# One core, a hybrid encoder layer: the order of long products, the buffers and the queues of its first stage

## The chip, the core and the metric

The kernel runs on one NeuronCore of a Trainium2 chip. The core's engines are TensorE (PE in the profile; PEld is its weight load), VectorE (DVE), ScalarE (ACT), GpSimd (POOL) and SyncE (SP). Each works through its own instructions in a fixed order and waits on semaphores for the others. SP does nothing but issue DMA copies here; POOL issues some, too, and computes beside them. The metric is the device time of one execution in microseconds, and the text compares medians of several executions.

## What is computed

One layer over a sequence of 2048 frames of width 1024. One input projection feeds two heads, their outputs are normalised and projected together, and a SwiGLU feed-forward part follows:

```python
h = rmsnorm(x, norm_mix_g[l])
proj = h @ w_in[l]
u_ssm = proj[..., :D_SSM]
q = proj[..., D_SSM:D_SSM + D_ATT]
...
y_ssm = s5_mixer(u_ssm, ...)
y_att = chunked_attention(q, k, v, attn_rel_bias[l])
mixed = jnp.concatenate([rmsnorm(y_ssm, ...), rmsnorm(y_att, ...)], axis=-1)
x = x + mixed @ w_out[l]
h2 = rmsnorm(x, norm_ffn_g[l])
x = x + (jax.nn.silu(h2 @ w_gate[l]) * (h2 @ w_up[l])) @ w_down[l]
return rmsnorm(x, norm_final_g)
```

The state-space head discretises a diagonal complex system first: `lam_bar = exp(lam * dt)`, with `b_bar`, powers of `lam_bar` and products of those powers with the matrices B and C. These tables depend on parameters alone. The attention head adds a learned bias that is clipped by distance; it reads it from a table of shape 8 x 128 x 640.

## The kernel before

All arithmetic is float32; each large product is made of three products of a high and a low part (`mm3`, line 144). Instructions are written with a tile framework: a builder orders them by priority (program order, moved by `high_priority`) and by its own estimate of when their inputs are there, allots buffers and sets the waits. A pool with `bufs=n` for a name gives n buffers in turn; the next user of one waits until all readers of the last are done. `keep_in_program_order` pins an instruction behind the one that was written just before it on its engine. All products of PE in this part are pinned, so PE's order is that of the program. The order on DVE, ACT, POOL and SP is fixed when the kernel is built, but by the builder's estimate.

The first stage, `u_phase` (line 395), projects x onto the 512 channels of the state-space head, in four blocks b of 512 columns. `prep` (line 410) loads the eight row tiles of a block (`xt`, from `in_xp`) on SP, splits each into a high part (ACT, line 424) and a low part (DVE, line 425), and loads the rows of x once more (`xn`) for the sums of squares. For block 0 it loads the weights as well. A block's four groups of 24 products on PE follow (`group`); between its first and its second group, `finish` (line 461) closes the block before: `spread_` turns the reciprocal norms into a row on PE and ACT (`pp`, `pb`), and four `evac` (line 450) multiply it in on DVE, into the buffers `us`, and store them to DRAM (`u`) on POOL's queue. The last block is closed after its fourth group.

The tables are made beside it, by the generator `ssm_prologue` (line 156), which `u_phase` and later the attention advance with `next(pro)`. Its first step issues nine loads on POOL's queue, its second computes the small tables on DVE (`exp_`, `poly`, sine and cosine, 128 x 16 elements each). Then come eight long products (`cmul`, line 267): four of 128 x 576 (`v`, stored to `vs` on POOL's queue) and four of 128 x 512 (`wt0`, `wt1`; called `wt` in the profile, as the copies below are). Each consists of six DVE operations of which two are pinned. LONG says how many of these steps follow the evacuation of blocks 0, 1 and 2: one, two and two; the other three follow the evacuation of block 3. After them POOL raises the table `a8` to powers, SP loads `bb` (`bbg`) and `v` back (`vg`, two of them in buffers called `bst`), and PE makes the kernels `kt` from them (`pp<-vg,bbg`), in program order among the first products of the attention.

The bias table (`nbms`, lines 484 to 488) is a copy from DRAM to DRAM of 8 x 128 rows of 2560 B, out of `nbs`, and two small copies that write 1e30 into corners; SP issues them in block 2. Attention reads it as `nb`.

The attention (`att_phase`, line 623) follows. Its pool `aw` lies where the first stage's pools lay. It loads and splits weights (`load_w`: `raw`, `w`) and x (`hT_unit`, lines 655 to 668), and its first q/k unit is the first work of PE after the first stage (`pf`). The feed-forward part begins at about 1000 us. Among its steps `weight_steps` (line 1166) prepares w_down; it first copies four of its blocks from DRAM to DRAM, 512 KB each (`wt`, line 1201), which the last part reads at about 2250 us. Nothing holds these four copies back, and the builder puts them early on SP's queue.

Of the kernel before, what the change touches and what calls it, by code (L numbers as in the profile page):

```python
# [61 lines left out]
DG = 3  # L62
DGROUPS = (3, 3, 3, 2), (3, 3, 3)
LATER = 230
LONG = 1, 2, 2
TAILF = 9, 10, 20, 21


# [87 lines left out]
def ssm_prologue(k, ident, S):  # L156
# [3 lines left out]
    with tc.tile_pool(name="pro", bufs=1) as p:  # L160
# [20 lines left out]
        def ts(in0, s1, s2=None, op0=ALU.mult, op1=ALU.add):  # L181
            o = sm()
            if s2 is None:
                V.tensor_scalar(o[:], in0[:], s1, None, op0=op0)
            else:
                V.tensor_scalar(o[:], in0[:], s1, s2, op0=op0, op1=op1)
            return o

        def tt(a, b, op):
            o = sm()  # L190
            V.tensor_tensor(o[:], a[:], b[:], op=op)
            return o
# [8 lines left out]
            return ts(m, MAGIC, None, ALU.subtract)  # L201

        def poly(r, cs):
            o = ts(r, cs[0], cs[1])
            for c in cs[2:]:
                o = tt(o, r, ALU.mult)
                o = ts(o, c, None, ALU.add)
            return o

        def pow2(kk):  # L210
# [5 lines left out]
        def exp_(x):  # L216
            x = ts(x, -104.0, 89.0, ALU.max, ALU.min)
            kk = rnd(x, 1.4426950408889634)
            r = stt(kk, -0.693359375, x, ALU.mult, ALU.add)
            r = stt(kk, 2.12194440e-4, r, ALU.mult, ALU.add)  # L220
            e = poly(r, [1 / 5040, 1 / 720, 1 / 120, 1 / 24, 1 / 6, 0.5, 1.0, 1.0])
            k1 = ts(kk, -100.0, 100.0, ALU.max, ALU.min)
            k2 = tt(kk, k1, ALU.subtract)
            a, b = pow2(k1), pow2(k2)
            o = sm()
            V.tensor_tensor(o[:], e[:], f32(a[:]), op=ALU.mult)
            o2 = sm()
            V.tensor_tensor(o2[:], o[:], f32(b[:]), op=ALU.mult)
            return o2
# [7 lines left out]
        r = stt(kk, -7.54978995489188216e-8, r, ALU.mult, ALU.add)  # L237
        r2 = tt(r, r, ALU.mult)
        sp = poly(r2, [2.7557319e-6, -1.9841270e-4, 8.3333333e-3, -1.6666667e-1])
        sp = tt(sp, r2, ALU.mult)  # L240
        sn = stt(sp, 1.0, r, ALU.mult, ALU.mult)
        sn = tt(sn, r, ALU.add)
        cp = poly(r2, [-2.7557319e-7, 2.4801587e-5, -1.3888889e-3, 4.1666667e-2])
        cp = tt(cp, r2, ALU.mult)
        cp = tt(cp, r2, ALU.mult)
        cs = stt(r2, -0.5, cp, ALU.mult, ALU.add)
        cs = ts(cs, 1.0, None, ALU.add)
# [118 lines left out]
        for b_ in range(4):  # L366
            nc.gpsimd.dma_start(S["kt"][:, 8 * b_ : 8 * b_ + 8, 0], kt[:])
        bb = k.t(p, "bbg", [P, NG, CH])
        nc.sync.dma_start(bb[:], S["bb"].rearrange("q g c n m -> (c n) (q g) m"))
        dm = k.t(p, "dm", [CH, NG, CH])  # L370
        V.tensor_tensor(dm[:], ident[:CH, :CH].unsqueeze(1).to_broadcast([CH, NG, CH]),
                        ddt[:].unsqueeze(2).to_broadcast([CH, NG, CH]), op=ALU.mult)
        vgs = []
        for b_ in range(4):
            vgs.append(k.t(p, "vg" if b_ < 2 else "bst", [P, 8, P], bufs=2))
            nc.sync.dma_start(vgs[b_][:], S["v"].rearrange("q g c n m -> (c n) (q g) m")[:, 8 * b_ : 8 * b_ + 8, :P])
        for b_ in range(4):
            gs = slice(8 * b_, 8 * b_ + 8)
            vg = vgs[b_]
# [15 lines left out]
def u_phase(k, ident, S):  # L395

    tc, nc, io = k.tc, k.nc, k.io
    with ExitStack() as cx:
        p2 = cx.enter_context(tc.tile_pool(name="u2", side="right", bufs=2))
        p1 = cx.enter_context(tc.tile_pool(name="u1", side="right", bufs=1))  # L400
        p3 = cx.enter_context(tc.tile_pool(name="u3", side="right", bufs=4))
        psum = cx.enter_context(tc.tile_pool(name="ups", bufs=6, space=bass.MemoryType.PSUM, reuse_waits="tile"))
        psum2 = cx.enter_context(tc.tile_pool(name="ups2", bufs=2, space=bass.MemoryType.PSUM, reuse_waits="tile"))
        k.pro_psum = psum2
        wh, wl = k.t(p1, "wuh", [P, KT, DS], F32R), k.t(p1, "wul", [P, KT, DS], F32R)
        rsn = S["rsn"][:].rearrange("p (c j) -> p j c", j=L)
        te = k.te
        X, ST, pbs = {}, {}, {}

        def prep(b, each=None):  # L410
            X[b] = []
            for q in range(KT):
                if b == 0:
                    if q % 2 == 0:
                        xn = k.t(p2, "xn", [P, D], bufs=3)
                    raw = xn[:, q % 2 * DS : q % 2 * DS + DS]
                    nc.sync.dma_start(raw, io["w_u"][q * P : (q + 1) * P, :])
                    nc.scalar.activation(wh[:, q, :], raw, AF.Copy, scale=k.gm[:, q : q + 1])
                    nc.vector.scalar_tensor_tensor(wl[:, q, :], raw, k.gm[:, q : q + 1], f32(wh[:, q, :]),
                                                   op0=ALU.mult, op1=ALU.subtract)  # L420
                xt = k.t(p3, "xt", [P, 512])
                nc.sync.dma_start(xt[:], io["xp"][q * P : (q + 1) * P, 2 * b : 2 * b + 2, :].rearrange("p j c -> p (j c)"))
                hi, lo = k.t(p2, f"hi{q}", [P, 512], F32R), k.t(p2, f"lo{q}", [P, 512], F32R)
                nc.scalar.copy(hi[:], xt[:])
                nc.vector.tensor_tensor(lo[:], xt[:], f32(hi[:]), op=ALU.subtract)
                X[b].append((hi, lo))
                if each:
                    each(q)
            ST[b] = ss = k.t(p2, "ss", [P, 4])
            for i in range(4):  # L430
                xn = k.t(p2, "xn", [P, D], bufs=3)
                nc.sync.dma_start(xn[:], io["x"].rearrange("(h p j) d -> j h p d", p=P, j=L)[2 * b + i // 2, i % 2])
                nc.scalar.activation(xn[:], xn[:], AF.Square, accum_out=ss[:, i : i + 1])

        def mm(b, f, ps, q):
            fs = slice(f * P, (f + 1) * P)
            mm3(te, ps[:], wh[:, q, fs], wl[:, q, fs], X[b][q][0][:], X[b][q][1][:], q == 0, q == KT - 1)

        def sums(b):
            with tc.high_priority():  # L440
                ST[b] = newton(k, p2, ST[b][:], D, 4)

        def spread_(b):
            ps = k.t(psum2, "pp", [P, 512])
            spread(k, te, ps, ST[b], 0)
            pbs[b] = pb = k.t(p1, "pb", [P, 512])
            nc.scalar.copy(pb[:], ps[:])
            nc.scalar.copy(rsn[:, 2 * b : 2 * b + 2, :], pb[:].rearrange("p (j c) -> p j c", j=2))

        def evac(b, f, ps):  # L450
            us = k.t(p3, "us", [P, 2, NC], bufs=2)
            nc.vector.tensor_tensor(us[:], ps[:].rearrange("p (j c) -> p j c", j=2), pbs[b][:].rearrange("p (j c) -> p j c", j=2), op=ALU.mult)
            nc.gpsimd.dma_start(S["u"][f * P : (f + 1) * P, 2 * b : 2 * b + 2, :], us[:])

        def group(b, f):
            ps = k.t(psum, "ps", [P, 512])
            for q in range(KT):
                mm(b, f, ps, q)
            return ps

        def finish(b, pss):
            with tc.high_priority():
                spread_(b)
                for f in range(4):
                    evac(b, f, pss[f])

        pss = [k.t(psum, "ps", [P, 512]) for _ in range(4)]

        def first(q):
            for f in range(4):  # L470
                mm(0, f, pss[f], q)

        pro = ssm_prologue(k, ident, S)

        next(pro)
        prep(0, first)
        with tc.high_priority(offset=-LATER):
            next(pro)
        sums(0)
        held = pss  # L480
        for b in range(1, 4):
            prep(b)
            if b == 2:
                corner = k.t(p1, "corner", [64, 64])
                nc.gpsimd.memset(corner[:], 1e30)
                nc.sync.dma_start(S["nbm"][:], bass.AP(S["nb"].tensor, S["nb"].offset + 1, [[768, H], [1, P], [1, 640]]))
                for m in range(2):
                    nc.sync.dma_start(S["nbm"][:, m * 64 : m * 64 + 64, m * 576 : m * 576 + 64].rearrange("h p c -> p h c"), corner[:].unsqueeze(1).to_broadcast([64, H, 64]))
            now = [group(b, 0)]
            finish(b - 1, held)  # L490
            for _ in range(LONG[b - 1]):
                next(pro)
            now += [group(b, 1), group(b, 2)]
            sums(b)
            held = now + [group(b, 3)]
        finish(3, held)
        for _ in range(8 - sum(LONG)):
            next(pro)
    return pro
# [666 lines left out]
def weight_steps(k, S, tile, tile1):  # L1166
# [31 lines left out]
        put(f, B22, a12)  # L1198

    for m, f in enumerate(TAILF):  # L1200
        nc.sync.dma_start(S["wt"][m], k.io["w_down"][f * P : (f + 1) * P, :])
    yield from in_turn(F2, load, first, second)


# [426 lines left out]
```

## Time and profile before

| | us |
|---|---|
| median of 3 runs | 2361.1 (2358.94 to 2367.68) |
| the profiled execution | 2359.18 |
| its span | 2357.4 |
| PE busy | 2209.4 (94%) |
| DVE busy | 1470.2 (62%) |
| POOL busy | 1140.1 (48%) |
| ACT busy | 1004.9 (43%) |
| mean clock granted to PE | 0.969 |

Times in the rows are from the start of the span. A timeline row has the start, the length, the engine, the line, the operation, output and inputs, shapes and a count; in brackets stands the idle time before it and what ended it. SPq is SP's queue: a row there is the time to issue a copy, not that of the copy. In a listing by groups stand the count, the busy time and the mean of one in nanoseconds, then the idle time before its instructions. In a list of copies stand the count, the size of one and the median from issue to landing.

### The profile page before, as it was taken

What the parts mean: (1) busy time and instruction counts of PE and PEld (TensorE: products, weight loads), DVE (VectorE), ACT (ScalarE), POOL (GpSimd) and SP (SyncE); (2) the same over time, 40 slices, a digit from 0 to 9 for tenths busy, and PEclk for the clock granted to TensorE, in tenths of its full rate; (3) what the DMA queues carried; (4) which work ended last, traced back from release to release, by engine and by line L of the source; (5) the groups of instructions that cost most, each with busy time, mean ns of one, the idle gap of its engine ahead of it and who ended that gap; (6) DMA issues with size and microseconds to landing.
All of it is one profiled execution on the core that took longest, in us unless ns stands there. A gap on an engine that the chain in (4) does not pass through costs nothing.

```text
span 2357.4 us, 30770 instructions
## 1 busy us (share of the span) xinstructions
PE 2209.4 (94%) x10712; PEld 1859.0 (79%) x10712; DVE 1470.2 (62%) x2247; ACT 1004.9 (43%) x1675; POOL 1140.1 (48%) x1284
## 2 busy tenths in 40 slices
PE   8958889999997899989999999999999989999996
PEld 6737788898986788768888887788888878888886
DVE  7554555756555845855775658766645375578676
ACT  5235545555556642333333334433333343345332
POOL 2245544556542423475555557655555464345442
PEclk9978999999998999999999999999999999999998
DMA  8876776765654434742544546654523187565541
GB/s 282 271 262 216 235 210 186 219 214 176 189 155 144 144 116 140 275 152 95 201 160 156 206 156 238 214 192 157 182 87 119 60 323 261 175 206 188 204 179 72
DMA packets 214195, 437.02 MB, mean 185 GB/s; under 512 B 27224, under 2 KB 57992, under 8 KB 206936
## 3 DMA queue, kind: packets, MB, share of 16 engines
q1 hardware_dynamic: 209176, 420.89, 53.8%
q0 software_dynamic: 4864, 14.17, 2.0%
q8 instruction: 84, 1.38, 0.2%
q14 instruction: 71, 0.58, 0.1%
HBM read 294.98 MB, written 132.15 MB: 181 GB/s over the span
## 4 chain that ended last, share of the span: by engine, by line
PE 75%; DVE 7%; DMA 7%; POOL 4%; issue 4%; ACT 2%; SPq 1%; DVEq 0%; POOLq 0%; ACTq 0%
PE X L76 19%; PE ps L76 19%; PE Y L76 9%; PE pf L76 8%; PE big L76 7%; PE W L76 5%; PE pj L76 4%; PE sc L76 2%; PE pt L79 2%; DMA xt<-in_xt 1%; DMA u<-us 1%; DMA lo<-hc 1%; DVE lo L153 1%; SPq L509 1%; DVE lo L668 1%
## 5 line engine op out<-in xcount | busy, mean ns | idle before, releaser
L76 PE MATMUL X<-hi,c 128*128 128x512 f32 x1408 | 450.6, 391 | 6.9 <-POOL c L153 3.5
L76 PE MATMUL ps<-hd,hd 128*128 128x512 f32 (+1 forms) x1968 | 433.8, 383 | 6.6 <-DVE hd L153 3.7
L76 PEld LDWEIGHTS ps<-hd,hd 128*128 128x128 f32 x1968 | 360.9, 191 | 78.2 <-DVE hd L153 4.1
L153 POOL TENSOR_TENSOR c<-S,c 128x512 fp32r<-128x512 f32 x176 | 253.1, 1439 | 240.9 <-ACT c L152 239.9
L76 PEld LDWEIGHTS X<-hi,c 128*128 128x128 f32 x1408 | 265.2, 188 | 64.2 <-POOL c L153 3.9
L153 POOL TENSOR_TENSOR hd<-hd 128x1536 fp32r<-128x1536 f32 (+1 forms) x53 | 188.7, 3568 | 208.1 <-ACT hd L152 194.3
L76 PE MATMUL X<-lo,c 128*128 128x512 f32 x704 | 274.4, 390 | 0.0
L153 POOL TENSOR_TENSOR c<-raw,c 128x512 fp32r<-128x512 f32 x132 | 190.4, 1443 | 132.7 <-ACT c L152 94.6
L152 ACT CAST hd<-hd 128x1536 fp32r<-128x1536 f32 (+1 forms) x106 | 147.4, 1393 | 225.1 <-DMA hd<-hq 154.3
L76 PE MATMUL Y<-hi,c 128*128 128x512 f32 x704 | 228.4, 395 | 13.6 <-DVE u L1320 13.6
L1444 DVE TENSOR_TENSOR acc<-acc,ps 128x512 f32<-128x512 f32 x196 | 129.1, 681 | 85.2 <-PE ps L76 85.0
L76 PEld LDWEIGHTS Y<-hi,c 128*128 128x128 f32 x704 | 134.4, 191 | 43.3 <-DVE u L1320 15.3
L76 PE MATMUL pf<-hi,w 128*128 128x512 f32 x416 | 154.3, 421 | 14.0 <-ACT hi L667 10.2
L76 PE MATMUL big<-m,woh 128*128 128x512 f32 x512 | 163.9, 402 | 0.2 <-DVE yr L986 0.2
L152 ACT CAST c<-S 128x512 fp32r<-128x512 f32 x176 | 109.4, 622 | 115.3 <-PE Y L76 59.6
L547 POOL TENSOR_TENSOR st<-X,a 128x128 f32<-128x128 f32 (+2 forms) x136 | 46.6, 343 | 229.8 <-ACT X L533 219.8
L781 DVE CUSTOM_DVE_ANT_0 s<-sc,nb 128x640 f32<-128x640 f32 (+4 forms) x128 | 94.5, 738 | 100.4 <-PE sc L76 96.3
L1316 ACT COPY u<-X 128x512 f32<-128x512 f32 x132 | 77.2, 586 | 183.7 <-PE X L76 183.7
L76 PEld LDWEIGHTS X<-lo,c 128*128 128x128 f32 x704 | 132.7, 188 | 27.6
L152 ACT CAST c<-raw 128x512 fp32r<-128x512 f32 x132 | 82.1, 622 | 152.7 <-PE Y L76 81.7
L76 PE MATMUL Y<-lo,c 128*128 128x512 f32 x352 | 138.8, 394 | 0.0
L153 DVE TENSOR_TENSOR hd<-hd 128x1536 fp32r<-128x1536 f32 (+1 forms) x53 | 114.7, 2166 | 34.0 <-ACT hd L152 33.2
(377 smaller groups left out, 4722.4 us busy)
## 6 DMA issues: line engine op xcount, KB each, us to landing
w<-wss SPq DMA_DIRECT2D x36, 1024.0 KB, 6.5
hq<-g SPq DMA_DIRECT2D x140, 256.0 KB, 2.0
hd<-hq SPq DMA_DIRECT2D x42, 768.0 KB, 4.5
hd<-wc SPq DMA_DIRECT2D x42, 768.0 KB, 6.1
raw<-in_w_gate SPq DMA_DIRECT2D x44, 512.0 KB, 3.7
raw<-in_w_up SPq DMA_DIRECT2D x44, 512.0 KB, 4.1
wc<-px SPq DMA_DIRECT2D x66, 256.0 KB, 2.7
wss<-w SPq DMA_DIRECT2D x12, 1024.0 KB, 5.3
```

The costliest lines, as they stand in the source:

```text
L76: return self.tc.keep_in_program_order(self.tc.nc.tensor.matmul(*a, **b))
L79: return self.tc.keep_in_program_order(self.tc.nc.tensor.transpose(*a, **b))
L152: nc.scalar.copy(hi, raw)
L153: (lo_eng or nc.gpsimd).tensor_tensor(lo, raw, f32(hi), op=ALU.subtract)
L509: ins = nc.sync.dma_start(out, in_)
L547: eng.tensor_tensor(t[:, :, :, :n], src, ar, op=ALU.mult)
L668: (nc.vector if sb or q % 2 == 0 else nc.gpsimd).tensor_tensor(lo[q][:], xt[:], f32(hi[q][:]), op=ALU.subtract)
L781: nc.vector.tensor_tensor_reduce(s[:, :nk].rearrange("p (a b) -> p a b", a=nch), ps[:, :nch, :half], hd.nb[:, nk - 1 :: -1].rearrange("p ( ...
L1316: nc.scalar.copy(u[:], ps[:])
L1444: V.tensor_tensor(a, a, ps[:], op=ALU.add)
```

## The change

Six edits, all but the last in the first stage:

- LONG becomes 1, 3, 4: three long products follow the evacuation of block 1, four that of block 2, none that of block 3.
- `us` has four buffers. For their room, `dm` moves into the buffer `cm1` of the long products.
- `poly` fuses the multiplication and the addition of a step into one operation; 14 small DVE operations fall away.
- The loads of `bb` and `v` are issued on POOL's queue.
- The bias table's copies are issued on POOL's queue, and stand behind the prologue's first loads, ahead of block 0.
- The four copies of w_down are pinned behind the SP instruction before them in the program.

```diff
-LONG = 1, 2, 2
+LONG = 1, 3, 4
...
         def poly(r, cs):
-            o = ts(r, cs[0], cs[1])
-            for c in cs[2:]:
-                o = tt(o, r, ALU.mult)
-                o = ts(o, c, None, ALU.add)
+
+            o = ts(r, cs[0], None)
+            for c in cs[1:]:
+                o = stt(o, c, r, ALU.add, ALU.mult)
             return o
...
-            e = poly(r, [1 / 5040, 1 / 720, 1 / 120, 1 / 24, 1 / 6, 0.5, 1.0, 1.0])
+            e = poly(r, [1 / 5040, 1 / 720, 1 / 120, 1 / 24, 1 / 6, 0.5, 1.0])
+            e = ts(e, 1.0, None, ALU.add)
...
-        sp = tt(sp, r2, ALU.mult)
...
-        cp = tt(cp, r2, ALU.mult)
...
-        nc.sync.dma_start(bb[:], S["bb"].rearrange("q g c n m -> (c n) (q g) m"))
-        dm = k.t(p, "dm", [CH, NG, CH])
-        V.tensor_tensor(dm[:], ident[:CH, :CH].unsqueeze(1).to_broadcast([CH, NG, CH]),
+        nc.gpsimd.dma_start(bb[:], S["bb"].rearrange("q g c n m -> (c n) (q g) m"))
+        dm = k.t(p, "cm1", [P, 576])[:CH, : NG * CH].rearrange("c (g m) -> c g m", g=NG)
+        V.tensor_tensor(dm, ident[:CH, :CH].unsqueeze(1).to_broadcast([CH, NG, CH]),
...
-            nc.sync.dma_start(vgs[b_][:], S["v"].rearrange("q g c n m -> (c n) (q g) m")[:, 8 * b_ : 8 * b_ + 8, :P])
+            nc.gpsimd.dma_start(vgs[b_][:], S["v"].rearrange("q g c n m -> (c n) (q g) m")[:, 8 * b_ : 8 * b_ + 8, :P])
...
-            us = k.t(p3, "us", [P, 2, NC], bufs=2)
+            us = k.t(p3, "us", [P, 2, NC])
...
         next(pro)
+        nc.gpsimd.dma_start(S["nbm"][:], bass.AP(S["nb"].tensor, S["nb"].offset + 1, [[768, H], [1, P], [1, 640]]))
+        corner = k.t(p1, "corner", [64, 64])
+        nc.gpsimd.memset(corner[:], 1e30)
+        for m in range(2):
+            nc.gpsimd.dma_start(S["nbm"][:, m * 64 : m * 64 + 64, m * 576 : m * 576 + 64].rearrange("h p c -> p h c"), corner[:].unsqueeze(1).to_broadcast([64, H, 64]))
         prep(0, first)
...
-            if b == 2:
-                corner = k.t(p1, "corner", [64, 64])
-                nc.gpsimd.memset(corner[:], 1e30)
-                nc.sync.dma_start(S["nbm"][:], bass.AP(S["nb"].tensor, S["nb"].offset + 1, [[768, H], [1, P], [1, 640]]))
-                for m in range(2):
-                    nc.sync.dma_start(S["nbm"][:, m * 64 : m * 64 + 64, m * 576 : m * 576 + 64].rearrange("h p c -> p h c"), corner[:].unsqueeze(1).to_broadcast([64, H, 64]))
...
-        nc.sync.dma_start(S["wt"][m], k.io["w_down"][f * P : (f + 1) * P, :])
+        k.tc.keep_in_program_order(nc.sync.dma_start(S["wt"][m], k.io["w_down"][f * P : (f + 1) * P, :]))
```

The function `stt(a, s, b, op0, op1)` is one DVE operation, `(a op0 s) op1 b`; `ts` and `tt` are one each, too. The pool of `us` has four buffers for a name where nothing else is said.

## The prediction

> **What bounds the kernel now.** I read the page first, then windows by stage, then the queue's waits and the timelines of the first stage.
>
> ```profile
> span 2357.4 us, 30770 instructions
> ...
> PE 75%; DVE 7%; DMA 7%; POOL 4%; issue 4%; ACT 2%; SPq 1%; DVEq 0%; POOLq 0%; ACTq 0%
> ```
>
> The chain of waits is three quarters TensorE (PE): from some 180 us on, little more than its own work holds it back. The first stage is different.
>
> ```profile
> 16.00:20.00 4.00, 4.00 (x19) 3.31 (x18) 2.72 (x8) 2.69 (x4) 0.00 (x0) 1.00 1.00 338
> 20.00:24.00 4.00, 4.00 (x19) 3.32 (x18) 4.00 (x13) 1.77 (x3) 0.00 (x0) 1.00 0.55 182
> 82.14:95.35 13.21, 8.90 (x25) 5.46 (x25) 6.90 (x11) 5.29 (x9) 1.54 (x3) 0.84 0.89 283
> 95.35:113.81 18.46, 18.46 (x81) 15.51 (x80) 9.89 (x27) 3.70 (x6) 4.73 (x8) 0.93 1.01 312
> 113.81:134.88 21.07, 5.67 (x42) 4.13 (x40) 12.70 (x20) 6.19 (x9) 2.31 (x5) 0.69 0.73 259
> 134.88:160.80 25.92, 22.01 (x96) 15.05 (x97) 18.82 (x26) 9.30 (x19) 12.68 (x13) 0.79 0.60 208
> 160.80:178.03 17.23, 8.64 (x48) 7.92 (x46) 6.80 (x11) 7.80 (x19) 13.67 (x40) 0.75 0.93 315
> 178.03:400.00 221.97, 198.98 (x1152) 175.64 (x1151) 119.15 (x259) 115.22 (x273) 112.42 (x264) 0.94 0.70 209
> 1030.00:1420.00 390.00, 384.99 (x1692) 317.54 (x1691) 252.57 (x279) 145.30 (x252) 212.10 (x148) 0.99 0.49 165
> ```
>
> The columns are the stretch, its length, then busy time of PE, PEld, DVE, ACT and POOL with counts, granted clock, DMA share and GB/s. From 178 to 400 PE works 199.0 of 222.0 us, from 1030 to 1420 385.0 of 390. From 113.81 to 134.88 it works 5.7 of 21.1, in the next 25.9 us 22.0 at a clock of 0.79, and from 82.14 to 95.35 8.9 of 13.2. These three holes are what the change can reach.
>
> The first hole is the bias table (nbms). Rows of SP's queue and what it waited for (total, times, longest):
>
> ```profile
> 52.50 0.87 SPq L486 DMA_DIRECT2D nbms<-nbs  x1
> ...
> 56.14 10.13 SPq L422 DMA_DIRECT2D xt<-in_xp  x1
> ...
> 77.37 1.38 SPq L488 DMA_DIRECT2D nbms<-corner  x2
> ...
> 100.60 3.70 SPq L1201 DMA_DIRECT2D wt<-in_w_down  x4
> ...
> 116.43 0.99 SPq L635 DMA_DIRECT2D raw<-in_w_qk  x2
> ```
>
> ```profile
> SPq L376 <- DMA vs<-v: 11.5, 1, 11.5
> ...
> SPq L488 <- DMA nbms<-nbs: 9.4, 1, 9.4
> ```
>
> ```profile
> 77.97 0.62 ACT L424 CAST hi<-xt 128x512 fp32r<-128x512 f32 x1 [10.54 <-DMA xt<-in_xp]
> ```
>
> The table's copy goes out at 52.50; the next x load needs 10.13 us to be issued, the corner copies then wait 9.4 us for the table, and all other loads stand behind them. Block 3's first columns reach ACT only at 77.97, after 10.54 us without work. PE sees it here:
>
> ```profile
> 41.84 1.05 PE L76 MATMUL pp<-ident,no 128*128 128x128 f32 x8
> ...
> 64.51 1.05 PE L76 MATMUL pp<-ident,no 128*128 128x128 f32 x8
> ...
> 84.58 0.79 PE L76 MATMUL ps<-lo,wuh 128*128 128x512 f32 x1 [2.44 <-DVE lo L425]
> ...
> 95.35 1.91 PE L76 MATMUL pp<-ident,no 128*128 128x128 f32 x8
> ...
> 113.81 1.05 PE L76 MATMUL pp<-ident,no 128*128 128x128 f32 x8
> ...
> 127.12 1.89 PE L76 MATMUL pp<-vg,bbg 128*16 128x128 f32 x8 [9.53 <-DVE us L452]
> ...
> 134.88 0.80 PE L76 MATMUL pf<-hi,w 128*128 128x512 f32 x1 [5.87 <-ACT hi L667]
> ```
>
> The second hole begins at the last spread (113.81). DVE's last evacuations stop for a store, because only two buffers exist, and ACT's first weight cast behind them stops too:
>
> ```profile
> 125.29 0.69 DVE L452 TENSOR_TENSOR us<-ps,pb 128x512 f32<-128x512 f32 x1 [7.76 <-DMA u<-us]
> ```
>
> ```profile
> 127.23 1.04 ACT L152 CAST w<-raw 128x1024 fp32r<-128x1024 f32 x1 [10.11 <-DVE us L452]
> ```
>
> So DVE lost 7.76 us, ACT 10.11, PE 9.53 and then 5.87. The third hole is DVE again: three long products lie between the last evacuation and the attention's own splits.
>
> **The change part by part.** The sum is made against the profiled execution, 2359.2 us: span 2357.4 and 1.8 around it. It lies 1.9 below the median of the three runs, 2361.1.
>
> ```profile
> 1085.34 5.44 PE X L76 x24
> ```
>
> *Term 1, block 3 no longer behind the bias table on SP.* 24 such products at full clock take 5.44 us. The 24 of block 3's first group took the 13.21 of its window (4.3 idle, the rest at a lower clock): 7.8 lost. The spread after them took 1.91 instead of the 1.05 of the one at 64.51: 0.9 more. I take -8.6. The other end is 0: three v products instead of two now stand on DVE behind the evacuation of block 1, and block 3's low parts behind them:
>
> ```profile
> L425 DVE TENSOR_TENSOR lo<-xt,hi 128x512 fp32r<-128x512 f32 x32 | 21.5, 684 | 6.9 <-ACT hi L424 6.9
> L452 DVE TENSOR_TENSOR us<-ps,pb 128x512 f32<-128x512 f32 x16 | 10.7, 688 | 23.3 <-DMA u<-us 19.1 <-ACT pb L447 4.1
> L285 DVE TENSOR_TENSOR v<-cm,cm 128x576 f32<-128x576 f32 x8 | 6.1, 757 | 0.1
> L285 DVE TENSOR_TENSOR wt<-cm,cm 128x512 f32<-128x512 f32 x8 | 5.5, 688 | 0.1
> ```
>
> A v product is 6 operations of 0.75 us (4.5), a wt product 6 of 0.69 (4.1), an evacuation 4 of 0.69. From 64.51 DVE needs some 4.5 for the spread's copy and evacuations, then 13.6: it is free at 82.6, and PE wants block 3 at 81.9 (64.51 + 1.05 + 3 x 5.44). If the eight low parts (5.5) come between the products, nothing is lost; if all come behind, PE trickles and the gain of this term is halved or worse.
>
> *Term 2, what the table costs at its new place.* POOL issues the prologue's loads until 12.4, and the table follows:
>
> ```profile
> 11.92 0.54 POOL L171 DMA_DIRECT2D ddt<-in_ssm_d  x1
> ...
> 42.73 1.66 POOL L333 DMA_DIRECT2D bbs<-bbr  x2 [26.76 <-DVE bbr L285]
> ```
>
> ```profile
> nbms<-nbs SPq DMA_DIRECT2D x1, 2560.0 KB
> ...
> wt<-in_w_down SPq DMA_DIRECT2D x4, 512.0 KB, 9.0
> ```
>
> POOL's wait for the table before the corner copies is hidden: its next work in the trace is at 42.73, after 26.76 idle, so a table of up to 25 us (52.5 to 77.4 as it was) costs POOL nothing; past that, bbs and the stores of u come late. The DMA engines are the price. 2560 KB are 2.62 MB; at the 338 GB/s of the row 16 to 20 that is 7.8 us, put among the loads of blocks 0 and 1, with a DMA share of 1.00 there. The row 20 to 24, share 0.55, has room for 1.8. So block 1's columns come 6 us later. Block 0's delay I take as hidden: PE is busy throughout both rows, so its columns are there ahead of it. But block 1 is tight now:
>
> ```profile
> 39.87 0.62 ACT L424 CAST hi<-xt 128x512 fp32r<-128x512 f32 x1 [0.87 <-DMA xt<-in_xp]
> ```
>
> ACT waits for its last column (0.87), and PE comes to the spread of block 0 at 41.84, right behind it. I take +6. Bounds: 0 if the room between SP's issues takes it all; +11.5 if the trickle also costs PE its clock, as the low-clock part of term 1's window did (13.21 - 4.3 - 5.44 = 3.5).
>
> On this the page "DMA: Bandwidth & Descriptors" of the Trainium skill speaks twice. Its section on SWDGE, HWDGE and iDMA says that DMAs issued from SP, ACT and POOL run on the same 16 engines, so that another issuing engine saves only the sequencer's issue time, usually small. Here that time was 10.13 and 9.4 us of SP, so the trace bears out the rule but not its "small"; taken strictly, the same bytes pass before block 3 as ever, terms 1 and 2 cancel, and the sum would be 2347. Its section on queues and rings says that an engine takes turns between its queues packet by packet; by that the SP loads run at half speed until the table is through, which is an estimate of 7.8 us later and 2346, and no row here shows the sharing.
>
> *Term 3, from the last spread to the attention's first product.* Before it is 134.88 - 113.81 = 21.07. With four evacuation buffers a store has a whole block's time to land, so the 7.76 go. The w_qk copies went out 2.6 after the spread, landing took 7.9:
>
> ```profile
> vg<-vs SPq DMA_DIRECT2D x2, 512.0 KB, 7.5
> ...
> raw<-in_w_qk SPq DMA_DIRECT2D x2, 512.0 KB, 7.9
> ```
>
> That makes 10.5, ACT's cast 1.04, the first x row on DVE (as a low part, 0.68) and its own cast (0.62): 12.8. So -8. Better end: the tail copies (4 x 512 KB, landing in 9.0) no longer run at 100.60; if that halves w_qk's landing, -12. Worse end: DVE now has four wt products (16.5), four evacuations (2.8) and a Newton chain (13 operations of 0.16) between the third and the last evacuation, 21.4 in a block time of 22.9 (4 x 5.44 + 1.05); if they don't fit, the last evacuation comes up to 3 later: -5.
>
> *Term 4, the first q/k unit.* 134.88 to 160.80 holds 18.8 of DVE, of which 11 operations of the moved long products, 7.6 us; without them DVE needs 11.2. PE's 22.0 at clock 0.79 would be 17.4 at full clock. I take 20: 25.9 - 20 = -6. Ends: -8.5 at full clock, 0 if POOL and ACT hold the unit as DVE did.
>
> *At nothing.* Polynomials: 14 operations fewer of 0.17 us at most, 2.4 us of DVE among loads that PE waits for on DMA. The dm product (0.67) waits for the last wt product now and is wanted only by the kt sums. bb and vg loads leave SP, where one waited 11.5 for vs; on POOL the same wait stands in front of later stores (a rival below). The tail copies, pinned behind the FFN's own steps, come to some 1244 us, where the DMA share of the stage is 0.49 and PE works 385 of 390; 2.1 MB at 338 GB/s delay the loads behind them on SP by 6.2 us, and weights lie one projection ahead. If that cover fails, up to 5. I take 0.
>
> *Sum:* -8.6 + 6 - 8 - 6 = -16.6, and 2359.2 - 16.6 = 2342.6; with the 1.9 up to the median, 2344.5: I say 2345. What follows only moves forward: nothing in it hangs on absolute time.
>
> **The rivals.**
> A, the table starves the first blocks: term 2 at +11.5, 2350. For it: DMA share 1.00 from 16 to 20 and PE's tight block 1. Against it: the room at 20.
> B, the table is hidden and the copies land early: term 2 at 0, term 3 at -12, sum -26.6, 2334.5. For it: 0.55 at 20 to 24. Against: 2.62 MB need 7.8, not 1.8.
> C, the gain is taken back at 160.80 to 178.03, where DMA is at 0.93 and PE works 8.6 of 17.2 for the loads of bias, u and weights: term 4 at 0 and 4 us more there, -6.6, 2354.5. Against: the tail copies' and table's bytes are gone by then.
> D, slower: POOL's queue takes over SP's stall. Its place is the vg load on POOL, which waits for a vs store as SP did for 11.5; behind it stand the stores of u and vs, and PE's kt products, in fixed order ahead of the q/k unit, wait for vg. A store waited for (11.5) and a landing after it (vg, 7.5) then stand in PE's way where terms 3 and 4 were to be earned: -8.6 + 6 + 11.5 + 7.5 = +16.4, 2377.5. It decides once a vg load lands later than about 14 us after the last spread (terms 3 and 4 together). Against: v's last product moves a block earlier, so its stores land long before.
> E, the builder's order puts the long products behind the last evacuation after all: term 4 is 0, 2350.
>
> **How the numbers follow.** Forecast 0.40, A 0.15, B 0.15, C 0.12, D 0.13, E 0.05. The forecast's own range is 2337 to 2352; to hold 8 in 10 it is stretched to 2329, most of B, and 2368, short of D. A measurement of this kernel can tell about 0.5%, 11.8 us, from no change: faster means below 2349.3, slower above 2372.9. Faster: forecast 0.34, B 0.15, A 0.07, E 0.02, C 0.02, together 0.60. Slower: most of D, 0.11. The same: 0.29.
>
> **What would show it.** Term 1: no SP wait for nbms, and block 3's first group in 5.5 to 6 us. Term 2: block 1's last column cast near 46 instead of 39.87, the spread of block 0 near 48. Term 3: no DVE wait for a store of u; the first pf product 13 us after the last spread. Term 4: the q/k unit in 20 us, with no long product in it. The tail copies near 1230 with no new hole in PE. It is wrong if PE's kt products wait for vg, if the last spread is not earlier than 112, or if the end moves by less than the start of the attention does.

## The result, and the profile after

The change makes the kernel slower: 2371.3 us (median of 22 runs) against 2361.0 (22 runs), a ratio of 1.0039 with a 95% interval of 1.0028 to 1.0051. The forecast was 2345, with a range of 2329 to 2368. The profiled execution took 2374.3 us, 3 above its median; that of before lies 1.8 below the median of these 22 runs. So the two traces differ by 15.1 us, 4.8 more than the medians.

The page of the changed kernel, its span and the chain of waits:

```profile
span 2372.5 us, 30747 instructions
...
PE 77%; DMA 7%; DVE 6%; POOL 4%; ACT 2%; issue 2%; SPq 1%; DVEq 0%; ACTq 0%; POOLq 0%
```

TensorE still sets the time. Windows of the first stage, cut at PE's own milestones (second spread, third, last, the attention's first product, the first transpose; columns as before):

```profile
71.77:105.57 33.80, 25.35 (x105) 20.57 (x104) 21.72 (x42) 8.26 (x14) 13.78 (x22) 0.85 0.63 176
105.57:122.89 17.32, 17.32 (x82) 14.45 (x81) 15.04 (x24) 1.82 (x2) 13.75 (x19) 1.00 0.55 152
122.89:140.42 17.53, 7.46 (x41) 5.28 (x39) 8.71 (x14) 6.42 (x9) 5.19 (x9) 0.69 1.02 334
140.42:155.52 15.10, 14.80 (x62) 9.34 (x63) 9.67 (x14) 6.44 (x11) 10.43 (x14) 0.79 0.71 237
```

From 71.77 to 105.57 PE works 25.4 of 33.8 us, and of these four stretches it works without a hole only in that from 105.57 to 122.89. PE's timeline says what it waits for:

```profile
39.39 0.79 PE L76 MATMUL ps<-hi,wuh 128*128 128x512 f32 x1 [6.61 <-ACT hi L423]
...
49.09 1.05 PE L76 MATMUL pp<-ident,no 128*128 128x128 f32 x8
...
86.75 0.77 PE L76 MATMUL ps<-hi,wuh 128*128 128x512 f32 x1 [8.45 <-DVE us L451]
...
122.89 1.05 PE L76 MATMUL pp<-ident,no 128*128 128x128 f32 x8
...
130.73 6.40 PE L76 MATMUL pp<-vg,bbg 128*16 128x128 f32 x32 [6.78 <-issue]
...
171.73 1.11 PE L79 MATMUL pp<-ident,wt 128*128 128x128 f32 x4 [7.82 <-ACT bst L292]
...
173.56 0.47 PE L76 MATMUL sc<-hi2x,hi0x 128*128 128x128 f32 x1 [0.71 <-ACT bst L292]
```

The first spread comes 7.3 us later than before (41.84), the last 9.1 later (113.81), the attention's first product 5.5 later (134.88), the first score product 5.7 later (167.82). Four waits are named: for block 1's columns (6.61), for an evacuation (8.45), for something that shows as "issue" ahead of the kt products (6.78), and for `bst` (7.82). Of the 15.1 us between the two profiles, 9.4 come behind the first score product.

The 6.61 is the table. In the list of copies and on POOL's timeline:

```profile
nbms<-nbs POOLq DMA_DIRECT2D x1, 2560.0 KB, 24.5
...
bbg<-bbs POOLq DMA_DIRECT2D x1, 256.0 KB, 10.8
```

```profile
13.90 1.12 POOL L475 DMA_DIRECT2D nbms<-nbs  x1 [1.47 <-DMA lr<-in_lam_re]
...
86.90 2.33 POOL L452 DMA_DIRECT2D u<-us  x4 [29.63 <-DVE us L451]
...
104.32 0.84 POOL L332 DMA_DIRECT2D bbs<-bbr  x1
...
116.70 0.99 POOL L375 DMA_DIRECT2D vg<-vs  x1
117.70 2.12 POOL L366 DMA_DIRECT2D kts<-kt  x4
119.81 1.73 POOL L368 DMA_DIRECT2D bbg<-bbs  x1
121.51 0.91 POOL L375 DMA_DIRECT2D vg<-vs  x1
...
128.13 1.79 POOL L375 DMA_DIRECT2D bst<-vs  x2
```

Issued at 13.90 it takes 24.5 us to land, all of it beside the loads of blocks 0 and 1. The lower rows belong to the 6.78: of the loads that the kt products read, `bbg` is issued only at 119.81, behind the stores of kt's zeros, and the second `vg` at 121.51. `bbg` takes 10.8 us to land, so it is there at 130.6, and the kt products start at 130.73. It can't be issued earlier, because it reads back what the `bbs` stores write: the first of these goes out at 104.32, the last at 112.55; in the kernel before the first went out at 42.73. Ahead of them POOL stands 29.63 us for the evacuation of block 1, whose stores of u come first in its order.

The 8.45 is on ACT and DVE, whose order is fixed when the kernel is built:

```profile
72.11 1.06 ACT L432 ACTIVATE xn<-xn 128x1024 f32<-128x1024 f32 x1 [1.83 <-DMA xn<-in_x]
...
75.64 1.96 ACT L423 CAST hi<-xt 128x512 fp32r<-128x512 f32 x3 [1.86 <-DMA xt<-in_xp]
78.24 1.06 ACT L432 ACTIVATE xn<-xn 128x1024 f32<-128x1024 f32 x1 [0.65 <-DMA xn<-in_x]
...
79.30 0.57 ACT L446 COPY pb<-pp 128x512 f32<-128x512 f32 x1
```

```profile
83.38 0.17 DVE L102 TENSOR_SCALAR nv<-ss 128x4 f32<-128x4 f32 x1 [0.82 <-ACT xn L432]
...
85.92 2.48 DVE L451 TENSOR_TENSOR us<-ps,pb 128x512 f32<-128x512 f32 x4
```

PE's spread of block 1 runs at 71.77, but ACT copies it (`pb`) only at 79.30, behind casts and squares of block 3 that wait for loads. DVE evacuates block 1 only at 85.92, behind low parts of block 3 and the start of block 3's Newton chain (83.38). The second group of products behind the spread, at 86.75, wants the PSUM buffer that this evacuation empties. In the kernel before the same copy ran 1.1 us behind its spread (64.51), ahead of block 3's first cast (77.97):

```profile
65.59 0.59 ACT L447 COPY pb<-pp 128x512 f32<-128x512 f32 x1 [3.06 <-PE pp L76]
...
77.97 0.62 ACT L424 CAST hi<-xt 128x512 fp32r<-128x512 f32 x1 [10.54 <-DMA xt<-in_xp]
```

The Trainium skill, "PSUM — Partial Sum Buffer", section on engine and sequencer instructions, calls the queues of ScalarE, VectorE and GpSimd strict first-in first-out; these rows agree (`pb` 7.5 us behind its input).

The 7.82 is POOL again. On ACT and on POOL:

```profile
171.30 1.20 ACT L292 COPY bst<-pp 128x256 f32<-128x256 f32 x4 [7.42 <-DMA bsts<-bst]
```

```profile
152.95 0.21 POOL L352 COPY a<-pr 128x16 f32<-128x16 f32 x1
...
166.59 0.32 POOL L283 TENSOR_TENSOR cp<-a 128x64 f32<-128x64 f32 x1
166.85 0.63 POOL L295 DMA_DIRECT2D bsts<-bst  x1
```

The copies of `bst` wait for a buffer whose store goes out at 166.85, behind POOL's chain of powers (from 152.95); before, it went out at 158.12.

### The profile page after: what moved, and what is told of

Its sections match the earlier page's. It is cut to its first block, busy times and chain, and to the rows that moved or that the text cites. A ratio compares the mean times of both kernels' runs of the same rounds, so it can differ in the third digit from the quotient of the medians.

```text
span 2372.5 us, 30747 instructions
## 1 busy us (share of the span) xinstructions
PE 2215.5 (93%) x10712; PEld 1865.1 (79%) x10712; DVE 1475.1 (62%) x2233; ACT 1004.7 (42%) x1675; POOL 1144.6 (48%) x1292
## 4 chain that ended last, share of the span: by engine, by line
PE 77%; DMA 7%; DVE 6%; POOL 4%; ACT 2%; issue 2%; SPq 1%; DVEq 0%; ACTq 0%; POOLq 0%
PE X L76 19%; PE ps L76 18%; PE Y L76 9%; PE pf L76 8%; PE big L76 8%; PE W L76 5%; PE pj L76 5%; PE sc L76 2%; PE pt L79 2%; DMA xn<-in_x 2%; DMA xt<-in_xt 1%; DVE lo L153 1%; SPq L507 1%; DMA hd<-wc 1%; POOL c L153 0%
## 5 line engine op out<-in xcount | busy, mean ns | idle before, releaser
L76 PEld LDWEIGHTS Y<-hi,c 128*128 128x128 f32 x704 | 134.3, 191 | 43.4 <-DVE u L1318 15.3
L76 PEld LDWEIGHTS X<-lo,c 128*128 128x128 f32 x704 | 132.5, 188 | 27.5
```

The source lines that it names most:

```text
L76: return self.tc.keep_in_program_order(self.tc.nc.tensor.matmul(*a, **b))
```

## The experiments

Fifteen kernels, each timed in the same rounds as the kernel before. Medians in us; the difference is to the median of before in the same runs, the ratio to its 95% interval. "Last spread" and "first product" (of the attention) are PE's starts in the profiled execution.

| kernel | time | difference | ratio | last spread | first product |
|---|---|---|---|---|---|
| before | 2361.0 | | | 113.8 | 134.9 |
| changed | 2371.3 | +10.3 | 1.0039 [1.0028, 1.0051] | 122.9 | 140.4 |
| before, tail copies late | 2365.0 | +3.3 | 1.0014 [0.9999, 1.0028] | 114.4 | 134.4 |
| before, table early on POOL | 2383.2 | +21.6 | 1.0092 [1.0069, 1.0114] | 133.6 | 152.3 |
| changed, table on SP in block 2 | 2360.3 | -1.4 | 0.9994 [0.9979, 1.0008] | 122.9 | 131.7 |
| changed, `bb` and `v` loads on SP | 2361.4 | -0.2 | 1.0008 [0.9995, 1.0022] | 123.6 | 132.5 |
| changed, both on SP | 2355.3 | -6.4 | 0.9978 [0.9960, 0.9996] | 116.1 | 125.4 |
| changed, old order of products | 2377.0 | +15.3 | 1.0074 [1.0052, 1.0096] | 121.6 | 141.3 |
| changed, table behind block 0's stores | 2372.7 | +11.5 | 1.0052 [1.0032, 1.0073] | 119.7 | 144.3 |
| changed, `bst` stores on SP | 2369.5 | +8.3 | 1.0033 [1.0018, 1.0048] | 123.4 | 138.5 |
| changed, block 3 pinned | 2359.3 | -2.4 | 0.9994 [0.9980, 1.0008] | 116.4 | 133.2 |
| block 3 pinned, loads on SP | 2357.9 | -4.3 | 0.9989 [0.9975, 1.0003] | 112.2 | 126.8 |
| the same, `bst` stores on SP | 2354.1 | -8.1 | 0.9964 [0.9949, 0.9980] | 112.6 | 125.9 |
| table, loads and `bst` stores on SP | 2350.7 | -11.5 | 0.9966 [0.9951, 0.9981] | 118.1 | 126.8 |
| table on SP in block 3 | 2353.2 | -8.0 | 0.9970 [0.9953, 0.9987] | 112.9 | 122.5 |
| the same, `bst` stores on SP | 2349.9 | -11.2 | 0.9954 [0.9940, 0.9969] | 115.0 | 124.6 |
| the same, block 3 pinned | 2365.8 | +4.1 | 1.0018 [1.0007, 1.0030] | 113.7 | 129.2 |

**One part alone, in the kernel before.** The tail copies pinned; the table moved as in the change.

```diff
-        nc.sync.dma_start(S["wt"][m], ...)
+        k.tc.keep_in_program_order(nc.sync.dma_start(S["wt"][m], ...))
```

> The kernel before with the four copies of w_down pinned late, nothing else. Both theories: no loss. 2.1 MB leave the stretch from 100 to 112 us, so the first weights land earlier: 2358 to 2361. A third theory, TAIL (the copies hurt where they are put now): 2365 or more, with new waits for raw or px near 1240 us.

> The kernel before with the bias table alone on POOL's queue ahead of block 0. Theory POOL: block 0's spread moves from 41.8 to about 49, block 3 no longer waits, and bbs, vs or bsts go out late on POOL; the end 2363 to 2370. Theory ORDER: the table by itself costs nothing or gains the 8.6 us of block 3's hole; 2352 to 2361.

An interval that holds 1.0000 means that the kernel can't be told from the one before; the difference and the ratio can then even differ in sign.

The tail copies bring nothing that can be measured. The table alone costs 21.6 us, more than either theory had. In that kernel, with two buffers, PE and DVE show:

```profile
86.48 0.76 PE L76 MATMUL ps<-hi,wuh 128*128 128x512 f32 x1 [18.77 <-DVE us L452]
```

```profile
56.22 0.68 DVE L452 TENSOR_TENSOR us<-ps,pb 128x512 f32<-128x512 f32 x1
...
85.65 1.28 DVE L452 TENSOR_TENSOR us<-ps,pb 128x512 f32<-128x512 f32 x2
```

Two of block 0's evacuations are done at 56, the other two at 85.65, behind the low parts of two blocks; PE stands 18.77 us. The first spread is already 8.5 us later than before (50.29 against 41.84), near theory POOL's 49; that is the price of the table's bytes. The larger part of the cost is this wait, and it comes from the place that DVE's order gives to the evacuations. Why the builder gave them that place is not shown.

**One part undone.** The changed kernel with the table back in block 2 on SP; with the loads back on SP; with both.

```diff
-        nc.gpsimd.dma_start(S["nbm"][:], ...)     # ahead of prep(0)
+                nc.sync.dma_start(S["nbm"][:], ...)     # if b == 2
```

```diff
-        nc.gpsimd.dma_start(bb[:], ...)
+        nc.sync.dma_start(bb[:], ...)
```

> The changed kernel with the bias table back on SP in block 2. Theory POOL (the table in front of the first blocks, and POOL's single queue, make the loss): block 0's spread is back near 42 us (49.1 in the changed kernel), block 3 waits for the table again, the end about 3 us below the changed kernel (2368). Theory ORDER (the evacuation of block 1 is placed behind block 3's data on ACT and DVE, which follows from the new LONG and the buffers): that wait stays, 8 us of PE, and the end is that of the changed kernel, 2371, or above.

> The changed kernel with the loads of bb and v back on SP. Theory POOL: the kt products no longer wait 6.8 us after the last spread, the first pf product comes 4 to 6 us earlier, the end near 2366. Theory ORDER: the kt products were late with the first stage, not because of the queue; the end stays at 2371.

> The changed kernel with both the table and the loads of bb and v back on SP's queue: what is left is the order of the long products, the four buffers, the polynomials and the late tail copies. ADDED (each queue edit costs its own 10 us): 2349 to 2353. SHARED (both act through the one queue of POOL, either undo alone mends it, and what is left after it is the same 8 us wait for bst): last spread near 123, the time 2357 to 2362.

Either undo wins back some 10 us, both together 16.0, so neither theory of the third kernel holds: not the whole sum, not one wait alone. With the table on SP its stall meets block 2 instead of block 3, and the last spread stays at 122.9:

```profile
79.11 0.79 PE L76 MATMUL ps<-hi,wuh 128*128 128x512 f32 x1 [12.60 <-ACT hi L423]
```

With the loads on SP the evacuation's wait stays, and the kt products start 1 us after the last spread (123.6), with no wait for vg or bbg:

```profile
88.03 0.76 PE L76 MATMUL ps<-hi,wuh 128*128 128x512 f32 x1 [6.45 <-DVE us L451]
...
124.56 2.79 PE L76 MATMUL pp<-vg,bbg 128*16 128x128 f32 x24
...
132.45 0.50 PE L76 MATMUL pf<-hi,w 128*128 128x512 f32 x1 [3.37 <-ACT hi L665]
```

From the last spread to the first product it is 8.9 us there and 8.8 with the table on SP, against 17.5 in the changed kernel. So with the table on SP the loads cost no wait although they stay on POOL. POOL's rows of that kernel show why:

```profile
36.76 1.66 POOL L332 DMA_DIRECT2D bbs<-bbr  x2 [19.82 <-DVE nf L109]
...
47.65 1.70 POOL L368 DMA_DIRECT2D bbg<-bbs  x1 [7.59 <-DMA bbs<-bbi]
```

The stores of `bb` go out at 36.76 instead of 104.32, and `bbg` at 47.65 instead of 119.81. With the loads on SP the stores are as late as in the changed kernel (105.62), but `bbg` is issued at 118.15 and lands in 4.3 us instead of 10.8. The two edits thus share one cost, the late `bbg`, and either undo removes it; this is why 11 and 10 add up to 16 only. The last spread comes earlier only with both undone (116.1).

**The order of the long products.** LONG back to 1, 2, 2.

> The changed kernel with the old order of the long products (one, two and two behind the first three evacuations, three behind the last). If the order earned what was forecast: from the first product of the attention to the first transpose PE needs 19 to 21 us instead of 15.1, and the time is 2374 to 2378. If the extra long products between the evacuations of blocks 1 and 2 are what makes the last spread late: last spread at 117 to 119 instead of 122.9, and the time 2364 to 2368. If both are so, they cancel: 2369 to 2373.

The time fits "the order earned what was forecast", the place doesn't: from the first product to the first transpose it takes 15.7 us, not 19 to 21. While PE waits for the loads of the kt products, DVE gets through 12 of the 18 operations of the last three long products; 6 fall into that unit. The order is worth some 5 us (2377.0 against 2371.3), but not in that unit: in the profiles 2.2 us lie between the last spread and the first product (19.7 against 17.5), where PE waits longer for the first cast of x, and 3.2 between the first and the second score product.

**Why the evacuation of block 1 is late.** First, the table pinned on POOL behind block 0's stores of u:

```diff
+                tc.keep_in_program_order(nc.gpsimd.dma_start(S["nbm"][:], ...))     # if b == 1, after finish(0)
```

> The changed kernel with the bias table still on POOL's queue, but pinned behind the four stores of block 0. QUEUE (the table's 2.6 MB stand ahead of the stores of u on POOL's queue, so the builder places the evacuations that reuse those buffers late): the stores of block 0 are ahead of the table now, so the evacuation of block 1 follows its spread at once, PE's wait of 8.45 for it is gone, the first spread is back near 42 and the last lies between 106 and 116, where block 3 pays for the table's bytes; the time 2355 to 2364. ORDER (the new order of the long products and the four buffers put that evacuation late, wherever the table is): the wait of some 8 us stays, the last spread is not earlier than 117, the time 2366 to 2372.

```profile
71.58 0.79 PE L76 MATMUL ps<-hi,wuh 128*128 128x512 f32 x1 [3.92 <-ACT hi L423]
...
75.69 1.91 PE L76 MATMUL pp<-ident,no 128*128 128x128 f32 x8
...
86.05 0.47 PE L76 MATMUL ps<-hi,wuh 128*128 128x512 f32 x1 [2.73 <-DVE us L451]
```

```profile
84.62 0.56 ACT L446 COPY pb<-pp 128x512 f32<-128x512 f32 x1
```

A miss for QUEUE: no store of block 0 is behind the table, yet ACT copies block 1's spread at 84.62, 8.9 after it. PE waits less for the evacuation (2.73) only because it has waited for casts of block 2 before (1.58 and 3.92). The time as a whole says little here: the stores of v now stand behind the corner copies on POOL, and the kt products wait 17.45 us. So the work that stands ahead of the evacuation was moved instead. Block 3 is written behind block 1's evacuation and its casts, low parts and squares are pinned; all queues stay as in the change:

```diff
-            prep(b)
+            if b < 3:
+                prep(b)
...
             finish(b - 1, held)
+            if b == 2:
+                prep(3)
...
+                if b == 3:
+                    tc.keep_in_program_order(high)
+                    tc.keep_in_program_order(low)
```

> The changed kernel, with the casts, low parts and squares of block 3 written behind the evacuation of block 1 and pinned there on ACT and DVE; queues as in the changed kernel. CAST ORDER (block 3's work stands ahead of the evacuation of block 1 on ACT and DVE, and waits there for loads): the evacuation of block 1 starts within 5 us of its spread (it was 14.15), PE's wait of 8.45 falls below 2, the last spread comes at 113 to 116 instead of 122.9, and the time is 2360 to 2367. TABLE (the data of block 3 themselves are late by the table's bytes): PE waits some 6 to 9 us for block 3's high part instead, the last spread stays at 120 to 124, the time 2368 to 2373. TAKEN BACK: the last spread is earlier, but PE's kt products wait for bbg and vg on POOL's queue and the transposes for bst by as much more; the time 2368 to 2373.

```profile
77.55 0.59 ACT L451 COPY pb<-pp 128x512 f32<-128x512 f32 x1 [5.52 <-PE pp L76]
```

```profile
78.17 2.48 DVE L456 TENSOR_TENSOR us<-ps,pb 128x512 f32<-128x512 f32 x4 [4.61 <-ACT pb L451]
```

CAST ORDER holds: with the spread at 76.5 the copy follows at 77.55 and the evacuation at 78.17 (1.7 us, not 14.15), PE has no wait of 1 us or more from the first spread (52.81) to the last (116.39), though the first is 3.7 later than in the changed kernel's profile, and the time falls by 12. Last spread and time lie just outside what was expected (113 to 116, 2360 to 2367), the one later, the other shorter. From the first spread to the last it takes 63.6 us, against 72.0 in the kernel before and 73.8 in the changed one. One rival is not separated: with block 3 written later, half of its x loads go out later as well (81.28 instead of 74.53), yet PE doesn't wait for them. Behind the last spread the kt products wait as in the changed kernel, and here the row names what for:

```profile
125.80 4.46 PE L76 MATMUL pp<-vg,bbg 128*16 128x128 f32 x21 [8.35 <-DMA vg<-vs]
```

**Whether the parts add.** Pins with the loads on SP, then the stores of `bst` on SP as well (`nc.sync` for `nc.gpsimd` in line 295 of the changed kernel), alone and with the others.

> The changed kernel with block 3's work pinned behind the evacuation of block 1, and the loads of bb and v back on SP's queue; the table stays early on POOL's queue. TWO TERMS (cast order and the kt products' wait for POOL's queue add up): last spread near 116, the first product of the attention 8 to 10 us behind it instead of 16.8, and the time is 2349 to 2353 (2359.3 less 7 to 10). ONE WAIT (the store of bst behind POOL's powers comes at its own time, and all that is gained ahead of it is lost there): the wait for bst grows from 7.3 to 12 or more, the time is 2357 to 2361.

```profile
72.20:112.20 40.00, 40.00 (x186) 33.26 (x185) 30.63 (x59) 12.49 (x20) 23.98 (x38) 1.00 0.85 240
```

```profile
165.32 0.47 PE L76 MATMUL sc<-hi2x,hi0x 128*128 128x128 f32 x1 [11.14 <-ACT bst L292]
```

The first row is what the forecast wanted: from the second spread to the last PE works 40.00 of 40.00 us at full clock. Yet the time is only 1.4 below the kernel with pins alone, so TWO TERMS missed, and ONE WAIT has the time. Most of what was gained is lost at the wait for `bst`, now 11.14 (ONE WAIT said 12 or more): the first product comes 6.4 us earlier than with pins alone, the first score product 2.2. From the last spread to the first product it still takes 14.7 us, not 8 to 10, because PE waits for an evacuation (4.08) and for the first cast of x (5.77).

> As the kernel before it, with the stores of bst on SP's queue too. If POOL's powers ahead of that store are a third term: the wait for bst falls under 3 us and the time is 4 to 8 us below the kernel before it, 2343 to 2348. If another wait stands right behind (the loads of the bias, u or weights): the same within 3 us.

> The changed kernel with the table, the loads of bb and v and the stores of bst all on SP's queue (POOL keeps the stores of u and v). By the third term: PE's wait of 7.80 at the transposes goes, the time is 4 to 8 us below the kernel with the first two on SP, 2347 to 2351. If not: 2353 to 2357.

> The changed kernel with nothing but the stores of bst moved to SP's queue. If POOL's chain of powers makes the 7.82 us wait at the transposes: that wait goes, PE's milestones up to the last product of kt stay as in the changed kernel (last spread near 123), and the time is 2363 to 2368. If the loss at the end is not there: 2370 to 2373, with another wait of the same size behind it (bias, weights or u on SP).

The wait at the transposes goes when the store leaves POOL, and the times fall by 3.8, by 4.6 and, in the changed kernel, by 1.8. Only the second lies where it was expected (2350.7, in 2347 to 2351); 2354.1 and 2369.5 lie between the two expectations of their kernels and meet neither. In all three a wait for `bst` of 5.2 us stands at the scores instead, as in the changed kernel with that one edit:

```profile
168.19 0.48 PE L76 MATMUL sc<-hi2x,hi0x 128*128 128x128 f32 x1 [5.21 <-ACT bst L292]
```

**The table behind all loads of x.** On SP again, but written in block 3:

```diff
-            if b == 2:
+            if b == 3:
```

> The changed kernel with the table on SP's queue, behind the last x load of block 3 instead of in block 2. QUEUE: no load of x and no store of u stands behind the table; spreads near 42, 65, 87 and 106 (87.4 + 18.46), no wait of PE for an evacuation, the first product of the attention near 118 to 124 (SP's copies of w_qk stand behind the table now), then the wait of some 8 us for the store of bst, later by what is gained; the time 2347 to 2354. ORDER: the last spread stays at 117 or later, the time 2359 or more. A third way, GIVEN BACK: the spreads as under QUEUE, but w_qk's copies or the loads after 160 are late by as much, the attention's first product not before 131; the time 2357 to 2362.

> As the kernel before it (table on SP behind block 3's loads), and the stores of bst on SP's queue instead of POOL's. If POOL's chain of powers in front of those stores is what PE's transposes wait for (7.82 us in the changed kernel), that wait goes to under 2 us and the time is 4 to 8 us below the kernel before it. If the four transposes are limited by the landing of the store itself, the wait stays above 5 us and the time is the same within 2 us.

> The same pins in the kernel with the table on SP behind block 3's loads and the stores of bst on SP. CAST ORDER: PE's wait of 4.04 for the evacuation of block 1 goes, the last spread comes at 109 to 112 instead of 115, and the time is 2345 to 2348. If nothing hangs on that order here: last spread 114 to 116, time 2349 to 2352.

The first two beat both kernels. The first has the time and the first product of QUEUE (2353.2, 122.5), but not its spreads: the last came at 112.9, not 106. The larger part of the 6.9 us is two waits for evacuations, 1.11 for block 0 and 3.36 for block 1, whose copy again stands behind block 3's casts on ACT (`pb` at 76.18, 8.4 after its spread):

```profile
77.61 0.73 PE L76 MATMUL ps<-hi,wuh 128*128 128x512 f32 x1 [3.36 <-DVE us L451]
```

What was won lies behind the last spread, 9.6 us to the first product; the loads of `bb` and `v` are on POOL there, too. Moving the stores of `bst` brings 3.2 us more, between the two expectations (4 to 8, or within 2): the wait at the transposes is 0.69, but 5.12 us are waited for at the scores.

The pins removed the wait for the evacuation as well (last spread 113.7 against 115.0), and the time is 16 us longer. With block 3 written later, the table went out at 68.34, ahead of block 3's last four loads of x; in the kernel without pins it went out at 76.90, behind all of them. DVE, pinned to block 3's low parts, stood for them:

```profile
68.34 0.79 SPq L491 DMA_DIRECT2D nbms<-nbs  x1
72.89 10.16 SPq L421 DMA_DIRECT2D xt<-in_xp  x4
```

```profile
91.64 2.68 DVE L424 TENSOR_TENSOR lo<-xt,hi 128x512 fp32r<-128x512 f32 x4 [16.37 <-ACT hi L423]
```

So most of three long products stood behind the last evacuation again, as before the change, and PE waited

```profile
129.15 0.80 PE L76 MATMUL pf<-hi,w 128*128 128x512 f32 x1 [9.05 <-ACT hi L674]
```

for the first cast of x, and 5.65 and 5.66 us later on. Both expectations for it missed. The edit moved the table as well as block 3's work, so it doesn't show what the pins alone would do.

## Why the prediction was wrong

- **Term 2, the table's price: right.** Forecast +6, measured +7.3 at the first spread, with the wait of 6.61 and the cast of block 1 where they were expected. The estimate by the Trainium skill ("DMA: Bandwidth & Descriptors", queues and rings: an engine takes turns between its queues) was 7.8.
- **Term 1, block 3 no longer behind the table: the failed step.** Forecast -8.6, measured +1.8 (122.89 - 49.09 against 113.81 - 41.84). SP's stall went as predicted. But it was argued that block 3's low parts would at worst come behind the long products and make PE trickle. They came ahead of the evacuation of block 1, and so did ACT's casts; all of them waited for loads, and PE waited 8.45 us for the PSUM buffer. The size was right: with the pins and every queue as in the change, the first spread to the last is 8.4 us shorter than before (63.6 against 72.0). And with the order repaired and the loads on SP, 49.3 us from the second spread to the last (113.81 - 64.51) became 40.0, which is -9.3. In time the pins alone took back 12 us. Why the builder put the casts there is argued, not shown: with SP's stall gone its estimate has block 3's data early, and in the kernel before, whose data come late, the evacuation stood ahead of them. With the table on SP in block 2, too, block 3's casts come behind the copy of block 1's spread, and no evacuation is waited for.
- **Term 3, last spread to first product: half, because "bb and vg at nothing" was wrong.** Forecast -8, measured -3.5. The wait for the store of u is gone (the last four evacuations are one row without idle time). But the loads on POOL stand behind POOL's other work, and the kt products wait 6.78 for them. This is rival D's place with another trigger and a smaller size: not a vs store of 11.5, but the stores of `bb`, which go out at 104.32 instead of 42.73, and so the late issue of `bbg`. It takes the table on POOL as well; with the table on SP the same loads cost nothing. With the loads on SP the term is -12.2 (8.9 against 21.07). That is the size of its better end, but by another way: the w_qk copies go out 3.9 us ahead of the last spread there, instead of 2.6 behind it. One number of the worse end was off: three groups of products lie between the third and the last evacuation, not four, so the room was 17.3 us and not 22.9. The products fitted all the same (the last evacuation comes 1.9 after its spread), because block 3's Newton chain was done at 86.
- **Term 4, the first q/k unit: right in size.** Forecast -6; from the first product to the first transpose 15.1 us against 20.0, -4.9. Its cause is not shown to be the order of the products: with the old order the unit takes 15.7. And the prediction overrated it: of the moved products 8 operations, 5.3 us, lie in that stretch of the kernel before, not 11 and 7.6.
- **What no term had:** the store of `bst` behind POOL's powers. It took most of the +5.1 between the first transpose and the first score product (18.03 us against 12.90). Rival C had a loss at that place, for loads, which is not what happened.
- **Polynomials, dm, tail copies: at nothing**, and nothing in the runs says otherwise for the tail copies (+3.3 alone); the other two were not tried alone.

Up to the first score product the measured terms are +7.25 + 1.83 - 3.54 - 4.93 + 5.13 = +5.74, against -16.6. Behind it the profiles differ by another 9.4. The two traces lie 4.8 further apart than the medians; if all of that falls behind the first score product, 4.6 remain. In the profiles 5.3 of the 9.4 arise between 287 and 322 us of the kernel before. There PE waits 4.39 us for `ptl` on DVE where it waited 1.29 before; why DVE is late is open. Two of the three signs that were named as proof against the forecast appeared: kt products that wait for their loads, and a last spread later than 112.

## What to carry to other kernels

When a stall is taken away, look at what the stalled data will now overtake: on an engine with a fixed order, work whose inputs are expected early is put ahead of work that another engine is waiting for, and if the inputs are then late, that engine waits for both. A copy moved to a compute engine's queue stands in that engine's program; count what is ahead of it there, and who waits for it. Place a large copy that nobody needs soon behind the loads that somebody needs now: the same table cost 21.6 us early on POOL in the kernel before, and with it behind block 3's loads on SP the changed kernel beats both.

## What was not expected of the hardware

The queue and the place of a copy in it decided far more than the time to issue it: 11 us with the table and 10 with the loads, each put back on SP alone (16 for both), and up to 11.14 us of PE's time for a store that stood behind computation on POOL. The Trainium skill, "DMA: Bandwidth & Descriptors", section on issuing engines, says that another issuing engine saves only the time to initiate a copy, which is usually small beside the copy itself. The rows agree: the table took 1.12 us to issue on POOL and 24.5 to land, `bbg` 1.73 and 10.8. What cost time here is what stood ahead of a copy on the engine that issues it; of that the sentence says nothing. The prediction held 10.13 and 9.4 us of SP against that rule, but these are the issue of the x load behind the table and a wait for the table's landing, not the time to initiate the table, which was 0.87.
